# Decay matrices of two DeltaNet pairs made in pieces inside the attention and kept in DRAM, first solve nearer to the attention

## The chip, the cores and the metric

The kernel runs on one core of one Trainium2 chip. The metric is the time of one execution in device microseconds, the median of several runs. A core has TensorE (PE, with its weight loads shown as PEld), VectorE (DVE), ScalarE (ACT), GpSimd (POOL), and SyncE (SP), which here only issues DMA transfers. Each works through its own list of instructions in order and waits on semaphores of the others. Data lies in on-chip SBUF (128 partitions), matmul results in PSUM, and inputs, outputs and spilled tiles in DRAM.

## The reference

One layer of a hybrid backbone, float32, for 512 latent tokens and 256 context tokens of width 1024. Cut to what matters:

```python
hx = modulate(rms_norm(x), sh1, sc1);  hc = modulate(rms_norm(ctx), csh1, csc1)
# (A) softmax attention, 8 query heads, 2 key heads, 512 queries against 256 + 512 keys
# (B) gated DeltaNet, 8 heads, chunks of 64 tokens, forwards and backwards, context first:
gam   = cumsum(log_a)                                  # within a chunk
dec   = exp(where(incl, gam[:, None] - gam[None, :], -inf))
kk    = k @ k.T                                        # within a chunk
a_mat = where(strict, beta[:, None] * dec * kk, 0) + eye(64)
u, w  = triangular_solve(a_mat, [beta * v, beta * exp(gam) * k])
# then a scan over the chunks: delta = u - w @ S;  S = exp(gam_last) * S + k_dec.T @ delta
#                              o = q_dec @ S + (dec * (q @ k.T)) @ delta
y = sigmoid(g_a) * (attn @ w_pa) + sigmoid(g_d) * (gdn @ w_pd);   x = x + g1 * (y @ w_out)
x = x + g2 * conv_ffn(modulate(rms_norm(x), sh2, sc2));  return rms_norm(x)
```

q, k and v of the DeltaNet come out of a projection, a centred convolution of width 3, silu, and for q and k a normalisation by head.

## The kernel before

A float32 matmul is made of three passes over operands split into a high and a low part (whi, wlo for weights; hxH, hxL for the latent and hcH, hcL for the context tokens). wraw is a weight tile as loaded, whi is written by ACT and wlo by VectorE.

The work goes through these stages: modulation and loads (0 to 75 us), projections for the attention (to 153), the attention (to about 325), the DeltaNet (to about 835), and the output projection and the FFN (to the end). Two long lists of independent TensorE work are cut into steps and put between the dependent parts. In the attention it is fillA, the first of the convolution projections (conv_proj, then tokens, which transposes the result co through PSUM tile xb and stores it as kTd, ktd, vtd). Behind it is fill: the other projections, z and gates, the projections pa and pd of the two branches. Asking a list for its next step is a pull; one pull of a projection is three matmuls of 128x512 or six of 128x256 into mb. The lists are fixed, so a pull that isn't taken early is taken later.

The attention (attend) goes through 32 units of 128 queries of one head, numbered u. A unit makes the scores into PSUM tile pS, of which there is one, the row maximum mx (VectorE), the exponentials pm (ACT), the normalisation of pm (VectorE), transposes into ab, their split PH (ACT) and PL (VectorE), and the products with the values. Between these stand pulls of fillA (F0 to F3 of them), and the order of TensorE is pinned as written. ACT, VectorE, POOL and SP are ordered by a scheduler, with contexts such as first() and sooner() as priorities.

The DeltaNet works on pairs of heads, p = 0 to 3. gdn_prep(p) loads k as kT, and makes the decay matrices NN: for each head, row blocks of gamdr are broadcast to all partitions for the two directions (NN and Gb, 128x768 each), POOL or VectorE adds a mask, ACT takes the exponential of six 128x128 pieces of each, and the two are added into NN. gdn_solve multiplies NN by pk = kT times kT and solves the diagonal 32x32 blocks on VectorE (C, X, and a chain of products prod and sums in R), which ends in o_tr and o_nt. gdn_inv makes the whole inverse from these on TensorE (pb), with copies into TTm and Tm on POOL and ACT. gdn_scan runs over the chunks; it loads vtok, ktok and masks M. The order of the first pair is written out:

```python
weave(wait(WK), 1.0)                                          # WK pulls
weave(gdn_solve(pre, G if 0 in SPOOL else V), RK)             # pk, NN times pk, the chain is issued
gdn_solved(pre, False)
weave(wait(W0), 1.0)                                          # W0 pulls, then gdn_inv(0)
```

The scheduler may put operations of gdn_prep ahead of the line at which they are written; their loads start at the attention's end, when the tiles' memory comes free.

Of the kernel before, what the change touches and what calls it, by code (L numbers as in the profile page):

```python
# [6 lines left out]
F32 = mybir.dt.float32  # L7
F32R = mybir.dt.float32r
AF = mybir.ActivationFunctionType
ALU = mybir.AluOpType  # L10
# [4 lines left out]
P = 128  # L15
D = 1024
# [12 lines left out]
NRM = "dve"  # L29
SOLVE = 2500000  # L30
POPS = (1, 3, 5, 7)
CHUNK, WK, W0, W1, RI, RS, RO = 1, 24, 66, 0, 3.0, 2.8, 2.0
RI0 = 2.4
NB = 6 - NX
POOLW = 0
KV = 10
GN = ''
FKS = '4466'
# [39 lines left out]
def hybrid_layer_body(tc, x, ctxt, xT, consts, cols, rows, w_mod1, w_mod2, w_av, w_aq, w_cm, w_pa, w_pd, w_out,  # L78
                      w_up, w_down, outT, dbg=None):
    nc = tc.nc  # L80
    V, A, G, SP = nc.vector, nc.scalar, nc.gpsimd, nc.sync
# [20 lines left out]
    def dump(name, ap):  # L102
        if dbg is not None and name in dbg:
            SP.dma_start(dbg[name], ap)

    def tt(out, a, b, op, eng=None):
        (eng or V).tensor_tensor(out=out, in0=a, in1=b, op=op)  # L107

    def ts(out, a, s1, op0, s2=None, op1=None, eng=None):
        if op1 is None:  # L110
# [5 lines left out]
        V.scalar_tensor_tensor(out=out, in0=a, scalar=s, in1=b, op0=op0, op1=op1)  # L116

    def act(out, a, f=AF.Copy, **kw):
        A.activation(out, a, f, **kw)  # L119

    def split(hi, lo, src):
        act(hi, src)
# [10 lines left out]
    with es:  # L133
        cp = es.enter_context(tc.tile_pool(name="cp", bufs=1))
        dp = es.enter_context(tc.tile_pool(name="dp", bufs=1, space=DRAM))
# [23 lines left out]
        msk_s = (cst[:, C_MS:C_MS + 128], cst[:, C_MS + 128:C_MS + 256])  # L159
# [38 lines left out]
        flat = lambda t: t.rearrange("p a b -> p (a b)")  # L198

        def load_w(src, nk=KT, pool=None, bufs=OH, n=None):  # L200
# [4 lines left out]
            with first() if pool is None else ExitStack():  # L205
                SP.dma_start(raw[:, 0:n], src)
                act(hi[:, 0:n], raw[:, 0:n])
                tt(lo[:, 0:n], raw[:, 0:n], hi[:, 0:n], ALU.subtract, G if pinned[0] and POOLW else V)
            return hi, lo
# [9 lines left out]
        gamdr = dp.tile([96, P], F32, name="gamdr")  # L219
        kTd = [dp.tile([P, NA], F32, name=f"kTd{i}") for i in range(NH)]  # L220
        qTd = [dp.tile([P, NL], F32, name=f"qTd{i}") for i in range(NH)]
        ktd = [dp.tile([P, NA], F32, name=f"ktd{i}") for i in range(NH)]
        vtd = [dp.tile([P, NA], F32, name=f"vtd{i}") for i in range(NH)]
        szd = [dp.tile([P, NL], F32, name=f"szd{i}") for i in range(NH)]
        atd = [dp.tile([P, NL], F32, name=f"atd{i}") for i in range(NH)]

        beta = cr.tile([P, 96], F32, name="beta")
        gam = cr.tile([P, 96], F32, name="gam")
# [201 lines left out]
        with m1_es:  # L430
# [11 lines left out]
            for op in LORD.split():  # L442
                i = int(op[1])
                with sooner():
# [3 lines left out]
                    elif op[0] == "h":  # L448
                        h, part = order[i]
# [312 lines left out]
        with at_es:  # L762
            at2 = at_es.enter_context(tc.tile_pool(name="at2", bufs=1, reuse_waits="tile"))
# [49 lines left out]
            def softmax(h, t, pS):  # L813
# [9 lines left out]
                    norm(pm, mx[:, 3:4])  # L823
                return pm

            def attend():
                U = 4 * NH
                at = lambda u: (u // 4, u % 4)
                pS, pms, pv = scores(0, 0), {}, None
                yield F0  # L830
                for u in range(U + 2):
                    if u < U:
                        pms[u] = softmax(*at(u), pS)
                    if u + 1 < U:
                        pS = scores(*at(u + 1))
                    yield F1
                    if pend:
                        columns(*pend.pop(0), xbank()[:, 0:2, :])
                    nxt = None
                    if 0 < u <= U:  # L840
                        nxt = probs(*at(u - 1), pms.pop(u - 1))
                    yield F2
                    if pv is not None:
                        pv()
                    yield F3
                    pv = nxt
# [30 lines left out]
        def gdn_prep(p, eng=G):  # L877
            kT = gq.tile([P, 2, NA], F32, name="kT", align_bytes=2048, tag="kT", bufs=2)
            for hh in range(2):
                SP.dma_start(kT[:, hh, :], kTd[2 * p + hh])  # L880
            g = gq.tile([P, 32], F32, name="g", tag="g", bufs=2)
            gT = gq.tile([P, 32], F32, name="gT", tag="gT", bufs=2)
            V.memset(g[:, 24:32], 0.0)
            for d in range(2):
                for hh in range(2):
                    r0 = d * 48 + (2 * p + hh) * 6
                    u = slice(12 * d + 6 * hh, 12 * d + 6 * hh + 6)
                    stt(g[:, u], beta[:, r0:r0 + 6], -1.0, rkk[2 * p + hh], ALU.mult, ALU.mult)
                    tt(g[:, u], g[:, u], rkk[2 * p + hh], ALU.mult)
            V.transpose(gT, g)  # L890
            NN = gq.tile([P, 12, P], F32, name="NN", align_bytes=2048, tag="NN", bufs=2)
            for hh in range(2):
                u = slice(6 * hh, 6 * hh + 6)
                Gb = gq.tile([P, 6, P], F32, name="Gb", tag="Gb", bufs=1)
                for d, D in ((0, NN[:, u, :]), (1, Gb)):
                    r0 = d * 48 + p * 12 + hh * 6
                    SP.dma_start(D.rearrange("p a b -> p (a b)"),
                                 gamdr[r0:r0 + 6, :].rearrange("a b -> (a b)").partition_broadcast(P))
                    tt(D, D, msk_s[d].unsqueeze(1).to_broadcast([P, 6, P]), ALU.add, eng)
                    for c in range(6):  # L900
                        act(D[:, c, :], D[:, c, :], AF.Exp, scale=-1.0, bias=gam[:, r0 + c:r0 + c + 1])
                tt(NN[:, u, :], NN[:, u, :], Gb, ALU.add, eng)
            return [kT, gT, NN]
# [427 lines left out]
        for p in range(NP):  # L1331
# [7 lines left out]
            out = (None, gdn_out(0), gdn_out(1), gdn_reload())[p]  # L1339
# [271 lines left out]
```

## Time and profile before

| | |
|---|---|
| runs | 1258.03, 1258.09, 1261.97 us; median 1258.09 |
| profiled execution | 1256.38 us, span 1254.5 us |
| mean granted clock of TensorE | 0.985 |
| busy: PE, DVE, ACT, POOL | 1196.7, 837.4, 613.8, 274.0 us |
| attention, 200 to 290 us | PE busy 90.00 of 90 us |
| behind it, 325 to 425 us | PE busy 86.10 of 100 us, clock 0.93 |

Times in the profile count from the first instruction. Busy is the sum of an engine's instruction times; a stall of TensorE shows as idle time before an instruction, with the instruction that ended it as releaser. The granted clock is the share of full speed at which the throttle lets TensorE run; at 0.5 a matmul takes twice its time. Line numbers (L107) are those of the kernel, and for helpers that all operations share they are the helper's: L86 matmul, L90 transpose, L107 tensor_tensor (L118 in the changed kernel), L116 scalar_tensor_tensor, L119 activation (L130).

### The profile page before, as it was taken

Reading aid. Unit: us, or ns where it says so; the run is one execution under the profiler, and the core shown is the slowest. Engines: PE = TensorE matmul, PEld = TensorE weight load, DVE = VectorE, ACT = ScalarE, POOL = GpSimd, SP = SyncE. Lnnn points to the kernel's source line nnn. Section 1 sums busy time; section 2 is a strip of 40 time slices with the busy share of each in tenths; the row PEclk is TensorE's granted clock in tenths of the full one; section 3 lists DMA queues with packets and bytes.
Section 4 is the critical chain, followed back from the end, with each engine's and each line's share of the span. In section 5 each row is a group of like instructions: output and inputs, shape, how many; then the busy total and the mean of one; then the engine's idle time right before and its main releaser. Section 6 shows DMA issues by size and latency. Waiting matters only on the chain. (4 is left out here: it accounts for less than half of the span.)

```text
span 1254.5 us, 20509 instructions
## 1 busy us (share of the span) xinstructions
PE 1196.7 (95%) x7733; PEld 1018.3 (81%) x7733; DVE 837.4 (67%) x1609; ACT 613.8 (49%) x1403; POOL 274.0 (22%) x347
## 2 busy tenths in 40 slices
PE   7999999999889899899999999899999999999996
PEld 3599879898778788778888778679888888888886
DVE  5767767777698866766757687855776766653333
ACT  6634466766675673773634632233544444442231
POOL 0120110110422387597484200210000000000000
PEclk9999999999999999999999999999999999999999
DMA  9412311211634533643546786854343332233331
GB/s 377 145 60 85 103 43 60 80 68 60 214 110 162 179 119 115 171 140 107 174 143 192 239 295 210 272 194 135 96 136 122 133 101 101 88 93 96 102 93 67
DMA packets 66403, 171.83 MB, mean 137 GB/s; under 512 B 7328, under 2 KB 18048, under 8 KB 64896
## 3 DMA queue, kind: packets, MB, share of 16 engines
q1 hardware_dynamic: 66304, 170.52, 41.0%
q8 instruction: 61, 1.00, 0.3%
q14 instruction: 38, 0.31, 0.1%
HBM read 145.28 MB, written 25.21 MB: 136 GB/s over the span
## 5 line engine op out<-in xcount | busy, mean ns | idle before, releaser
L107 DVE TENSOR_TENSOR wlo<-wraw,whi 128x1024 fp32r<-128x1024 f32 (+1 forms) x153 | 192.2, 1257 | 155.7 <-ACT whi L119 155.5
L119 ACT ACTIVATE whi<-wraw 128x1024 fp32r<-128x1024 f32 (+1 forms) x153 | 159.6, 1044 | 219.3 <-PE mc L86 112.5
L86 PE MATMUL mc<-h,whi 128*128 128x512 f32 (+1 forms) x752 | 219.7, 376 | 0.3 <-ACT whi L119 0.3
L86 PE MATMUL mb<-hxH,whi 128*128 128x512 f32 x384 | 162.3, 423 | 3.4 <-DVE R L107 2.8
L86 PEld LDWEIGHTS mc<-h,whi 128*128 128x128 f32 x752 | 138.0, 188 | 25.8 <-ACT whi L119 0.5
L86 PE MATMUL mb<-hxH,wlo 128*128 128x512 f32 x384 | 152.6, 397 | 0.0
L86 PE MATMUL mb<-hxL,whi 128*128 128x512 f32 x384 | 151.7, 395 | 0.0
L86 PE MATMUL mc<-h,wlo 128*128 128x512 f32 (+1 forms) x376 | 141.4, 376 | 0.5 <-DVE wlo L107 0.5
L86 PE MATMUL mc<-a,whi 128*128 128x512 f32 (+1 forms) x396 | 111.1, 367 | 0.6 <-DVE x L116 0.6
L107 POOL TENSOR_TENSOR rc<-rc,mhalf 128x2 f32<-128x2 f32 x4 | 3.3, 813 | 407.5 <-DVE rc L113 407.5
L86 PEld LDWEIGHTS mb<-hxH,wlo 128*128 128x128 f32 x384 | 72.9, 190 | 16.5
L86 PEld LDWEIGHTS mb<-hxH,whi 128*128 128x128 f32 x384 | 73.5, 191 | 13.7 <-issue 2.9
L86 PEld LDWEIGHTS mc<-h,wlo 128*128 128x128 f32 x376 | 70.8, 188 | 13.8 <-DVE wlo L107 1.0
L86 PEld LDWEIGHTS mc<-a,whi 128*128 128x128 f32 x396 | 71.6, 189 | 12.8 <-DVE x L116 0.8
L86 PEld LDWEIGHTS mb<-hxL,whi 128*128 128x128 f32 x384 | 73.5, 191 | 9.6
L86 PE MATMUL mc<-a,wlo 128*128 128x512 f32 (+1 forms) x198 | 72.4, 366 | 0.0
L116 DVE SCALAR_TENSOR_TENSOR u<-mc,col,u 128x511 f32<-128x511 f32 x88 | 65.3, 746 | 1.4
L107 POOL TENSOR_TENSOR prod<-X,R 128x31 f32<-128x31 f32 (+15 forms) x93 | 54.4, 584 | 20.6 <-DVE X L107 13.9
L107 POOL TENSOR_TENSOR R<-R,prod 128x31 f32<-128x31 f32 (+15 forms) x93 | 57.1, 614 | 7.0
L86 PE MATMUL pq<-whi,hxH 128*128 128x256 f32 (+1 forms) x192 | 55.6, 290 | 0.0
L86 PE MATMUL pq<-wlo,hxH 128*128 128x256 f32 (+1 forms) x192 | 54.4, 283 | 0.1
L86 PE MATMUL pq<-whi,hxL 128*128 128x256 f32 (+1 forms) x192 | 54.3, 283 | 0.0
(329 smaller groups left out, 2768.1 us busy)
## 6 DMA issues: line engine op xcount, KB each, us to landing
wraw<-in_w_cm_dram SPq DMA_DIRECT2D x48, 512.0 KB, 3.6
wraw<-in_w_up_dram SPq DMA_DIRECT2D x44, 512.0 KB, 3.3
wl<-in_w_mod_dram SPq DMA_DIRECT2D x24, 512.0 KB, 4.6
wm<-in_w_mod_dram SPq DMA_DIRECT2D x8, 1024.0 KB, 10.7
wraw<-in_w_down_dram SPq DMA_DIRECT2D x16, 512.0 KB, 3.5
wraw<-in_w_aq_dram SPq DMA_DIRECT2D x10, 512.0 KB, 3.7
M<-gamdr SPq DMA_DIRECT2D x64, 64.0 KB, 4.9
wraw<-in_w_pa_dram SPq DMA_DIRECT2D x8, 512.0 KB, 4.4
```

The costliest lines, as they stand in the source:

```text
L86: i = nc.tensor.matmul(*a, **k)
L107: (eng or V).tensor_tensor(out=out, in0=a, in1=b, op=op)
L116: V.scalar_tensor_tensor(out=out, in0=a, scalar=s, in1=b, op0=op0, op1=op1)
L119: A.activation(out, a, f, **kw)
```

## The change

The NN matrices of the first ND = 4 heads (pairs 0 and 1) are made during the attention, in tiles of their own, NN0 and Gb0 (NN_2056 and Gb_2057 in the rows below). Each head has two broadcast loads and two masks on POOL, then six pieces of two exponentials (DN = 2), one piece per unit, then a merge on POOL and a store to a DRAM tile nnd. These instructions are pinned in the order written. gdn_prep then loads NN of these heads from nnd and makes no masks or exponentials for them. WK goes from 24 to 10 and W0 from 66 to 60.

```diff
-CHUNK, WK, W0, W1, RI, RS, RO = 1, 24, 66, 0, 3.0, 2.8, 2.0
+CHUNK, WK, W0, W1, RI, RS, RO = 1, 10, 60, 0, 3.0, 2.8, 2.0
...
+ND, DN = 4, 2
...
+    def put(i):
+        return tc.keep_in_program_order(i) if strict[0] else i
...
+    def in_order(fn, *a):
+        strict[0] = True
+        fn(*a)
+        strict[0] = False
...
-        (eng or V).tensor_tensor(out=out, in0=a, in1=b, op=op)
+        put((eng or V).tensor_tensor(out=out, in0=a, in1=b, op=op))
...
-        A.activation(out, a, f, **kw)
+        put(A.activation(out, a, f, **kw))
...
+        nnd = [dp.tile([P, 6 * P], F32, name=f"nnd{i}") for i in range(ND)]
...
+            def decays():
+                NN = at2.tile([P, 6, P], F32, name="NN0")
+                Gb = at2.tile([P, 6, P], F32, name="Gb0")
+                rows6 = lambda d, h: slice(d * 48 + h * 6, d * 48 + h * 6 + 6)
+                def masks(D, d, h):
+                    SP.dma_start(D.rearrange("p a b -> p (a b)"),
+                                 gamdr[rows6(d, h), :].rearrange("a b -> (a b)").partition_broadcast(P))
+                    tt(D, D, msk_s[d].unsqueeze(1).to_broadcast([P, 6, P]), ALU.add, G)
+                def decay(D, d, h, c0):
+                    for c in range(c0, c0 + DN):
+                        kc = rows6(d, h).start + c
+                        act(D[:, c, :], D[:, c, :], AF.Exp, scale=-1.0, bias=gam[:, kc:kc + 1])
+                def merge(h):
+                    tt(NN, NN, Gb, ALU.add, G)
+                    SP.dma_start(nnd[h], NN.rearrange("p a b -> p (a b)"))
+                for h in range(ND):
+                    yield 0, lambda: masks(NN, 0, h)
+                    yield 0, lambda: masks(Gb, 1, h)
+                    yield 1, lambda: None
+                    for D, d in ((NN, 0), (Gb, 1)):
+                        for c in range(0, 6, DN):
+                            yield 1, lambda: decay(D, d, h, c)
+                    yield 0, lambda: merge(h)
+            pieces, left = decays(), [0.0]
+            def decay_pieces():
+                left[0] += 1
+                while left[0] > 0:
+                    share, fn = next(pieces, (99, None))
+                    left[0] -= share
+                    if fn:
+                        in_order(fn)
...
+                        decay_pieces()
...
+                if 2 * p + hh < ND:
+                    SP.dma_start(flat(NN[:, u, :]), nnd[2 * p + hh])
+                    continue
```

ACT in the attention, before: a unit's splits PH, then pm, with the transposed convolution output co between.

```order
L119 ACTIVATE ao<-ab 128x256
L119 ACTIVATE co<-t_2163 128x768
L119 ACTIVATE PH<-ab 128x4x128
L119 ACTIVATE PH<-ab 128x2x128
L119 ACTIVATE pm,mx<-pS,mx,qsc_174 128x768
L119 ACTIVATE co<-xb,hk_165 128x128 x4
L119 ACTIVATE PH<-ab 128x4x128
L119 ACTIVATE pm,mx<-pS,mx,qsc_174 128x768
L119 ACTIVATE PH<-ab 128x2x128
```

ACT in the attention, changed, over two units.

```order
L130 ACTIVATE PH<-ab 128x4x128
L130 ACTIVATE PH<-ab 128x2x128
L130 ACTIVATE Gb_2057<-Gb_2057,gam 128x128 x2
L130 ACTIVATE pm,mx<-pS,mx,qsc_178 128x768
L130 ACTIVATE ao<-ab 128x256
L130 ACTIVATE co<-t_2175 128x768
L130 ACTIVATE PH<-ab 128x4x128
L130 ACTIVATE PH<-ab 128x2x128
L130 ACTIVATE pm,mx<-pS,mx,qsc_178 128x768
```

A piece of two exponentials now stands behind the PH splits of a unit; in 11 of the 24 units with a piece it is directly ahead of pm, in the others behind it.

TensorE around pk, before: pk of pair 0 stands behind a whole projection of the context.

```order
L86 MATMUL mb<-hcH,whi 128x256
L86 MATMUL mb<-hcL,whi 128x256
L86 MATMUL mb<-hcH,wlo 128x256
L86 MATMUL pk<-kT 128x128 x4
L86 MATMUL mb<-hxH,whi 128x512
L86 MATMUL mb<-hxL,whi 128x512
L86 MATMUL mb<-hxH,wlo 128x512
L86 MATMUL pk<-kT 128x128 x2
```

TensorE around pk, changed.

```order
L91 MATMUL xb<-cst,co 128x128 x2
L87 MATMUL pk<-kT 128x128 x4
L87 MATMUL mb<-hcH,whi 128x256
L87 MATMUL mb<-hcL,whi 128x256
L87 MATMUL mb<-hcH,wlo 128x256
L87 MATMUL mb<-hcH,whi 128x256
L87 MATMUL mb<-hcL,whi 128x256
L87 MATMUL mb<-hcH,wlo 128x256
L87 MATMUL pk<-kT 128x128 x2
```

pk stands 14 pulls nearer to the attention, inside the projection that stood ahead of it; between pk and the inverse there are six pulls and six transposes fewer.

POOL ahead of and in the inverse of pair 0, before: all masks of M, then the copies of the inverse.

```order
L107 TENSOR_TENSOR M_5230<-M_5230,cst 128x256 x2
L107 TENSOR_TENSOR M_5241<-M_5241,cst 128x256 x2
L107 TENSOR_TENSOR M_5252<-M_5252,cst 128x256 x2
L107 TENSOR_TENSOR M_5263<-M_5263,cst 128x256 x2
L972 COPY TTm<-o_tr 32x12x32 x4
L972 COPY TTm<-o_nt 32x12x32 x4
```

POOL there, changed.

```order
L118 TENSOR_TENSOR M_5144<-M_5144,cst 128x256
L1027 COPY TTm<-o_tr 32x12x32 x4
L118 TENSOR_TENSOR M_5144<-M_5144,cst 128x256
L118 TENSOR_TENSOR M_5155<-M_5155,cst 128x256 x2
L1027 COPY TTm<-o_nt 32x12x32 x4
L979 MEMSET C 128x32x8
L118 TENSOR_TENSOR M_5166<-M_5166,cst 128x256 x2
L118 TENSOR_TENSOR M_5177<-M_5177,cst 128x256 x2
```

The copies of o_tr and o_nt stand among the masks of M, whose operands come by DMA.

1 line of the change is left out of this document (added).

## The prediction

> **What bounds the kernel now.** I read the stretches of the span first, then the waits of TensorE, then the work in front of those waits. Columns of the stretch table: length, then busy time (and instructions) of PE, PEld, DVE, ACT, POOL, then the granted clock, the DMA share and GB/s.
>
> ```profile
> 200.00:290.00 90.00, 90.00 (x609) 81.16 (x608) 68.53 (x135) 58.81 (x146) 6.96 (x4) 1.00 0.20 68
> 325.00:350.00 25.00, 21.88 (x122) 18.83 (x120) 15.11 (x46) 19.58 (x64) 11.02 (x6) 0.93 0.68 221
> 325.00:425.00 100.00, 86.10 (x544) 73.12 (x543) 83.40 (x167) 68.87 (x193) 40.46 (x35) 0.93 0.52 170
> 349.40:417.40 68.00, 58.77 (x310) 49.02 (x308) 63.57 (x116) 43.86 (x114) 23.10 (x19) 0.95 0.46 149
> 700.00:775.00 75.00, 70.87 (x477) 59.03 (x476) 60.04 (x129) 26.66 (x54) 0.78 (x1) 1.00 0.80 259
> 900.00:1254.00 354.00, 345.08 (x1595) 288.62 (x1593) 193.11 (x264) 132.13 (x180) 1.39 (x2) 0.99 0.33 106
> ```
>
> TensorE sets the time. Inside the attention (200 to 290) it is never idle, with POOL at 6.96 of 90 us; from 900 on it misses 9 us in 354. Behind the attention, 325 to 425, it is idle 13.9 of 100 us, and a granted clock of 0.93 costs some 7 us more. About 21 us are to be had there. Some of its waits there, and pk (start, duration, instruction; in brackets the idle time before it and its releaser):
>
> ```profile
> 344.24 1.11 PE L90 MATMUL xb<-cst,co 128*128 128x128 f32 x4 [2.94 <-DVE co L116]
> ...
> 348.28 1.05 PE L86 MATMUL pk<-kT 128*128 128x128 f32 x8
> ...
> 364.91 0.76 PE L86 MATMUL mb<-hxH,whi 128*128 128x512 f32 x1 [2.76 <-DVE R L107]
> ...
> 417.43 0.24 PE L86 MATMUL pb<-o_tr,NN 32*32 32x32 f32 x2 [1.12 <-DVE o_tr L952]
> ```
>
> Two halves meet at pk (348.28). Ahead of it the fill's pulls run while ACT and POOL make the decay matrices; the convolution's co stands behind exponentials on ACT, and TensorE waits 2.94 us for the co that follows from it. Behind pk, VectorE runs the solve of pair 0 (NN times pk, X, the R chain, o_tr) with the fill's own VectorE work in between, 63.57 of 68.00 us busy, and the first product of the inverse (417.43) waits for its o_tr. The operations that the change touches, and what they do to VectorE:
>
> ```profile
> 339.69 1.85 ACT L119 ACTIVATE NN<-NN,gam 128x128 f32<-128x128 f32 x6
> 341.45 0.83 ACT L119 ACTIVATE co<-t 128x768 f32<-128x768 f32 x1
> ```
>
> ```profile
> 360.40 1.84 POOL L107 TENSOR_TENSOR NN<-NN,Gb 128x768 f32<-128x768 f32 x1 [2.63 <-ACT Gb L119]
> 366.19 1.82 POOL L107 TENSOR_TENSOR Gb<-Gb,cst 128x768 f32<-128x768 f32 x1 [3.95 <-DMA Gb<-gamdr]
> 371.43 1.84 POOL L107 TENSOR_TENSOR NN<-NN,Gb 128x768 f32<-128x768 f32 x1 [3.42 <-ACT Gb L119]
> ```
>
> ```profile
> 349.98 0.95 DVE L107 TENSOR_TENSOR NN<-NN,Gb 128x768 f32<-128x768 f32 x1
> ...
> 360.57 2.75 DVE L107 TENSOR_TENSOR X<-X,gT 128x1024 f32<-128x1024 f32 x1
> ...
> 371.47 1.98 DVE L107 TENSOR_TENSOR R<-R,prod 128x156 f32<-128x156 f32 x1
> 373.48 0.34 DVE L107 TENSOR_TENSOR prod<-X,R 128x175 f32<-128x175 f32 x1
> ...
> 414.12 1.22 DVE L947 TENSOR_TENSOR R<-R,gT 128x1024 f32<-128x1024 f32 x1
> ```
>
> A VectorE operation that meets a wide one of POOL is held by it: beside the merge at 360.40, X*gT takes 2.75 against the 1.22 of the same shape at 414.12, and beside the one at 371.43 an R step takes 1.98 where a wider step takes 0.34.
>
> **The change part by part.** The sum is made against the profiled execution, 1256.38 us; the median of the runs, 1258.09, stands 1.7 above it.
>
> ```profile
> 204.12 0.87 ACT L119 ACTIVATE PH<-ab 128x512 fp32r<-128x512 f32 x2 [1.77 <-PE ab L90]
> 204.87 0.99 ACT L119 ACTIVATE pm<-pS,mx,qsc 128x768 f32<-128x768 f32 x1
> ```
>
> ```profile
> 204.83 0.39 PE L86 MATMUL mb<-hxH,whi 128*128 128x512 f32 x1
> 205.07 0.39 PE L86 MATMUL mb<-hxL,whi 128*128 128x512 f32 x1
> 205.29 0.40 PE L86 MATMUL mb<-hxH,wlo 128*128 128x512 f32 x1
> 205.52 0.60 PE L90 MATMUL xb<-cst,co 128*128 128x128 f32 x4
> 206.01 0.50 PE L86 MATMUL pS<-KH,QH 128*128 128x512 f32 x1
> ```
>
> *Exponentials in the attention.* Two per unit, 2 x 0.31 = 0.62 us (1.85 for six), in 24 units. ACT has room (58.81 of 90 us), but pS has one buffer: the next scores start when ACT has read pm out of it. In the unit shown pm ends at 205.86 and the scores start at 206.01, a slack of 0.15 us. The new order puts the pair directly ahead of pm in 11 of the 24 units. Units of the shape shown (both PH splits ahead of pm) come once in four, so I count 6 that lose 0.62 - 0.15 = 0.47 us, and nothing for the others, which have ACT's idle time (1.77 us ahead of the PH row) to take it: 6 x 0.47 = +2.8, taken as +3. The ends are 0 and 11 x 0.62 = +7.
>
> *Masks, merges, loads and stores in the attention.* Twelve POOL operations of 1.82 us or more on an engine that is 92% free there cost TensorE nothing of themselves; VectorE can be held by them up to 1.5 us each, and has 21.5 of 90 us idle. I take 0 for them, since only an operation with little slack behind it passes a hold on; the bad end is the rival below. On SP, 8 loads and 4 stores of 384 KB join a stretch with a DMA share of 0.20. A store waits for its merge, and the load of the next weights stands behind it on SP, so that it comes a merge (1.84 us) late at most, four times; no row of the attention shows TensorE short of weights, so 0. The next head's first exponential waits for merge, store, load and mask, whose parts are 1.84 + 2.3 + 6.0 + 1.84 = 12.0 us by the POOL rows and these landings (kTd<-co for a store, kT for a load of the same size, in a crowded stretch). Two units last ten, since a normalisation, one per unit, comes 18 times in 90 us (row below). So ACT may stand 2 us, twice; most units absorb it, and the bounds above hold it.
>
> ```profile
> kT<-kTd SPq DMA_DIRECT2D x4, 384.0 KB, 6.0
> NN<-gamdr SPq DMA_DIRECT2D x4, 384.0 KB, 8.1
> ...
> kTd<-co SPq DMA_DIRECT2D x1, 384.0 KB, 2.3
> ```
>
> *24 pulls to 10 ahead of pk.* A pull is three matmuls, 0.69 us (204.83 to 205.52). pk comes 14 x 0.69 = 9.7 sooner, and the wait of 2.94 goes with the exponentials that caused it, with 1.7 of half clock (0.07 of the 25 us to 350): 14.3, so pk at 333.9. The 24 pulls, that wait and that clock account for 21 us ahead of 348.28, so the attention ends at 325 to 327 and kT and NN have 7 to 9 us to land. The loads above took 6.0 and 8.1 where nine queued; nine queue now, but pk's first products need only kT and the first two of NN. I take no wait.
>
> *pk to the inverse.* It took 417.43 - 348.28 = 69.2. Two bounds. TensorE's own work: 58.77 less 3.4 for the clock of 0.95, plus pk, less 6 pulls and a group of six transposes (5.0), is 51.5. The VectorE chain: 68.0 unchanged at worst; less the two holds shown (1.53 + 1.64), the merge (0.95), some 2 for the fill's VectorE work in six pulls (an estimate: a third of 63.57 us over 66 pulls) and about 4 of other holds, by the mask at 366.19 and the scan's, and of VectorE's 4.4 us of idle time: 58. I take 58, because VectorE was 93% busy there and remains the longer of the two. So the inverse starts at 333.9 + 1.1 + 58 = 393.0, 24.4 sooner. But 20 pulls and six transposes, 13.8 + 0.9 = 14.7 us of TensorE work, have only been moved behind it. Net -9.7; the ends are +0.3 (the chain stays at 68) and -17 (only TensorE's work counts). What is late next is o_tr: TensorE will stand 7 to 8 us before the inverse.
>
> *The inverse and scan 0.* Their fill is 20 pulls nearer, and SP's queue puts the scan's loads behind a store and a load of that fill:
>
> ```profile
> 401.06 6.15 SPq L1034 DMA_DIRECT2D M<-gamdr  x10
> ```
>
> They began 16 us ahead of the inverse; with 14.7 us of fill gone it would be 1 to 2, plus the 7 to 8 of waiting. On POOL the masks of M now stand among the copies TTm<-o_tr and TTm<-o_nt that the inverse needs. The loads fit while TensorE waits. +0.5, ends 0 and +4.
>
> *The tail.* The 20 pulls come out at the end of the fill, beside the projections that move most data (700 to 775: DMA share 0.80, TensorE 4.1 us idle). Another 14.7 us at that stretch's idle share (4.1 of 75) cost 0.8, at five times that share 4; waits of the later projections may go as well: +1, ends -2 and +4.
>
> Sum: +3 - 9.7 + 0.5 + 1 = -5.2: 1251.2 in a profiled execution, 1252.9 as median.
>
> [...]
>
> **The rivals.**
>
> *Slower: POOL holds the attention.* The normalisation of pm stands between softmax and the transposes once a unit:
>
> ```profile
> L111 DVE TENSOR_SCALAR pm<-pm,mx 128x768 f32<-128x768 f32 x18 | 11.2, 621 | 0.6
> ```
>
> It takes 0.62, and no wide POOL operation ran beside it. Stretched to 1.84 in each of the twelve masks and merges, and on the path each time, it would add 12 x 1.2 = 14 us: -5.2 becomes +9, 1267. Without the attention the sum is -8.2, so the kernel gets slower by over 0.3% from 12 us lost in the attention, 0.5 us in each of 24 units. For it: the holds are real. Against it: VectorE has a quarter of its time free there, and POOL would be busy with them 22 of some 120 us, so most normalisations meet none. Chance 0.13, from 1262 up.
>
> *Given back: the chain doesn't shrink.* If VectorE's solve takes its 68 us with less fill to cover it, the stretch gives +0.3 and the sum is +4.8 at the worst, half way back it is 0: 1258 to 1263. For it: the fill's own VectorE work is interleaved by the scheduler and may just close up around the chain. Against: the holds at 360, 366 and 371 have lost their POOL partner. Chance 0.17.
>
> *More: TensorE's work alone counts.* If the chain ends within the fill, -17 with the attention (+3), the tail (+1) and the M loads (0.5 to 4) is -9 to -12.5: 1245.6 to 1249. Chance 0.25.
>
> **How the numbers follow.** Forecast 0.45, with a range of its own from 1249 to 1257. From the four cases: faster by over 0.3% (3.8 us, about what a measurement of this kernel can tell) is all of the larger gain and two thirds of the forecast, 0.57; within 0.3%, 0.25; slower by more, most of the contention case and a part of the giving back, 0.18. The range, 1243 to 1261, takes in the forecast, the larger gain and the giving back, and leaves out the contention case.
>
> **What would show it.** Right: 24 pairs of exponentials on ACT in the attention, TensorE waiting for pm some 0.5 us in a few units and otherwise full; pk about 14 us sooner, with no wait for co ahead of it; X*gT at 1.22; one wait of 5 to 9 us for o_tr ahead of the inverse. Wrong: normalisations of 1.2 us and more beside POOL rows; a wait for NN from nnd; waits for TTm or M inside the inverse; new waits for weights between 780 and 840.

## The result, and the profile after

| | median us | runs | range |
|---|---|---|---|
| before | 1258.44 | 7 | 1256.84 to 1262.52 |
| changed | 1267.33 | 7 | 1264.15 to 1270.71 |

The changed kernel is slower by 0.6%: the ratio is 1.0062, with an interval of 1.004 to 1.0085. 1252.9 was forecast. The profiled execution took 1269.64 us (span 1267.6), 2.3 above its median, and that of before 1256.38 (span 1254.5), 2 below its own; so about 9 of the 13.1 us between the spans are the change. In the experiments below, disturbed executions (one each of m_place and s_swap_16_74) are left out.

TensorE does the same work (busy 1196.8 us, before 1196.7), so the 13 us are idle time and must be looked for stage by stage. The stage table of the changed kernel; columns are the length, busy time and count of PE, PEld, DVE, ACT, POOL, then granted clock, DMA share, GB/s. The stages are the attention, its end to inverse 0, inverse 0 to inverse 3, inverse 3 to the output projection, and the rest:

```profile
153.44:333.54 180.10, 169.41 (x1117) 149.35 (x1117) 133.81 (x246) 123.41 (x330) 38.34 (x24) 0.99 0.27 91
333.54:402.20 68.66, 59.19 (x357) 51.31 (x355) 58.50 (x150) 39.34 (x102) 14.90 (x12) 0.97 0.53 182
402.20:678.74 276.54, 265.35 (x2281) 227.45 (x2281) 186.25 (x358) 151.70 (x405) 183.24 (x267) 0.98 0.44 139
678.74:844.96 166.22, 149.41 (x993) 122.81 (x993) 112.12 (x212) 60.94 (x135) 24.02 (x22) 0.97 0.69 230
844.96:1267.60 422.64, 412.33 (x2035) 349.72 (x2033) 234.90 (x342) 160.13 (x228) 5.11 (x5) 0.99 0.34 109
```

The same of before:

```profile
153.56:325.31 171.75, 167.47 (x1117) 150.13 (x1117) 125.67 (x246) 110.52 (x282) 16.70 (x12) 0.98 0.19 68
325.31:417.43 92.12, 79.74 (x426) 67.36 (x424) 78.11 (x160) 62.86 (x177) 34.12 (x25) 0.94 0.52 169
417.43:688.48 271.05, 261.57 (x2268) 224.68 (x2268) 186.68 (x359) 147.74 (x390) 179.05 (x263) 0.99 0.46 148
688.48:831.78 143.30, 134.75 (x936) 110.08 (x936) 107.21 (x208) 53.36 (x122) 21.22 (x19) 0.99 0.75 245
```

The stages changed by +8.3, -23.5, +5.5, +22.9 and -0.1 us. The counts of matmuls say how much of this is work that only moved: the second stage has 69 fewer, the third 13 and the fourth 57 more. A fill matmul starts 0.23 us after the one before (three take 0.69 us, 204.83 to 205.52, in the profile of before), so 13.1 of the fourth stage's 22.9 us are moved work. The third stage's 13 are three fill matmuls and ten transposes of 0.1 us (four take 0.36 us, 414.32 to 414.68, in the profile of before), about 1.7 us of its 5.5. What is new is 8 us in the attention, 10 us in the fourth stage and 4 us in the third, against the 9 that the second stage gained beyond its moved work. In the fourth stage TensorE's busy time grows by 14.7 us (149.41 against 134.75) for 13.1 of moved work, so 1.5 of its extra 9.8 us are longer matmuls and 8.3 are idle time.

The steps at TensorE, from the timeline of the changed kernel (start, duration, instruction, in brackets the idle time before and its releaser):

```profile
341.30 0.94 PE L87 MATMUL pk<-kT 128*128 128x128 f32 x7
...
402.20 0.31 PE L87 MATMUL pb<-o_tr,NN 32*32 32x32 f32 x2 [7.58 <-DVE o_tr L1007]
...
683.32 0.25 PE L87 MATMUL pb<-o_nt,NN 32*32 32x32 f32 x1 [4.33 <-DVE oacc L118]
...
785.03 0.92 PE L91 MATMUL pb<-cst,oacc 128*128 128x128 f32 x4 [2.23 <-DVE oacc L122]
...
821.19 0.71 PE L87 MATMUL mb<-g_s,whi 128*128 128x512 f32 x2 [4.37 <-DVE gd L127]
```

pk comes 7.8 us behind the attention's end without a wait, and the first product of the inverse waits 7.58 for o_tr, as forecast. The last three rows are waits of the fourth stage, which held 8.55 us of idle time before and 16.81 now.

### The profile page after: what moved, and what is told of

The parts are those of the page before. It is cut to its first block, busy times and chain, and to the rows that moved or that the text cites. A ratio compares the mean times of both kernels' runs of the same rounds, so it can differ in the third digit from the quotient of the medians.

```text
span 1267.6 us, 20507 instructions
## 1 busy us (share of the span) xinstructions
PE 1196.8 (94%) x7733; PEld 1017.4 (80%) x7733; DVE 830.4 (66%) x1603; ACT 614.4 (48%) x1403; POOL 283.0 (22%) x353
## 4 chain that ended last, share of the span: by engine, by line
PE 73%; DMA 8%; DVE 7%; ACT 5%; POOL 3%; issue 3%; SPq 1%; POOLq 0%; DVEq 0%; ACTq 0%
PE mc L87 32%; PE mb L87 19%; PE pq L87 6%; PE pb L87 6%; PE pS L87 2%; PE ab L87 2%; DMA NN<-gamdr 2%; POOL NN L118 1%; PE pm L87 1%; DMA Gb<-gamdr 1%; DMA wl<-in_w_mod_dram 1%; DVE wlo L118 1%; DMA gt<-atd 1%; PE ab L91 1%; ACT pm L130 1%
## 5 line engine op out<-in xcount | busy, mean ns | idle before, releaser
L118 DVE TENSOR_TENSOR wlo<-wraw,whi 128x1024 fp32r<-128x1024 f32 (+1 forms) x153 | 189.6, 1240 | 163.8 <-ACT whi L130 156.3
L87 PE MATMUL mb<-hxL,whi 128*128 128x512 f32 x384 | 152.9, 398 | 0.0
L87 PEld LDWEIGHTS mb<-hxH,whi 128*128 128x128 f32 x384 | 74.1, 193 | 10.6
L87 PEld LDWEIGHTS mc<-a,whi 128*128 128x128 f32 x396 | 71.6, 189 | 12.9 <-DVE x L127 0.8
L118 POOL TENSOR_TENSOR R<-R,prod 128x31 f32<-128x31 f32 (+15 forms) x93 | 59.9, 644 | 6.7
```

The lines of the kernel that those rows point to most:

```text
L87: i = nc.tensor.matmul(*a, **k)
L118: put((eng or V).tensor_tensor(out=out, in0=a, in1=b, op=op))
```

## The experiments

Each profile was cut into the same stages. The table has stage lengths of one profiled execution each, the matmuls of the fourth stage in brackets, and the time: median and ratio to before, or one execution where no ratio stands.

| kernel | attention | to inverse 0 | to inverse 3 | to output projection | us | ratio |
|---|---|---|---|---|---|---|
| before | 171.8 | 92.1 | 271.1 | 143.3 (936) | 1258.4 | |
| changed | 180.1 | 68.7 | 276.5 | 166.2 (993) | 1267.3 | 1.0062 |
| a_fill_only | 170.5 | 84.6 | 277.1 | 165.3 (994) | 1278.0 | 1.0151 [1.0103, 1.0199] |
| b_masks_only | 177.6 | 80.3 | 273.1 | 143.0 (937) | 1255.6 | 0.9971 [0.995, 0.9992] |
| c_w0_80 | 179.1 | 84.1 | 267.9 | 143.9 (936) | 1254.7 | 0.9969 [0.995, 0.9988] |
| d_w1_5 | 179.2 | 68.6 | 280.8 | 153.9 (948) | 1261.2 | 1.0019 [1.0002, 1.0036] |
| e_swap | 177.0 | 81.0 | 271.5 | 145.2 | 1254.1 | 0.997 [0.9946, 0.9993] |
| f_no_pool | 176.1 | 89.2 | 273.4 | 145.7 | 1262.8 | |
| g_no_exp | 176.2 | 91.0 | 273.3 | 143.1 | 1262.7 | |
| h_w0_70 | 179.1 | 70.5 | 279.4 | 160.6 (965) | 1265.2 | 1.0049 [1.0028, 1.007] |
| j_no_wl_loads | 179.4 | 68.7 | 274.9 | 156.0 (993) | 1256.2 | |
| k_w0_80_no_wl_loads | 178.9 | 84.7 | 268.8 | 137.9 (936) | 1250.9 | |
| m_place | 178.8 | 81.9 | 273.8 | 146.1 | 1256.5 | 0.9977 [0.9954, 0.9999] |
| n_dma_only | 175.9 | 90.1 | 273.5 | 143.7 | 1260.7 | |
| o_no_m_loads | 179.1 | 71.6 | 278.2 | 162.9 (993) | 1269.2 | |
| p_w0_80_no_m_loads | 177.3 | 86.7 | 265.6 | 148.1 | 1254.7 | |
| q_dve | 180.2 | 80.1 | 272.1 | 142.6 | 1258.9 | 1.001 [0.9989, 1.0031] |
| r_dve_place | 186.6 | 81.1 | 276.2 | 143.8 | 1261.9 | 1.0034 [1.0016, 1.0052] |
| s_swap_16_74 | 179.2 | 86.2 | 269.9 | 144.0 | 1260.6 | 1.0022 [1.0002, 1.0042] |
| t_w0_90 | 179.0 | 91.1 | 267.2 | 150.8 (906) | 1266.6 | 1.0074 [1.0051, 1.0096] |

**The two parts apart.** First the moved fill without the early matrices:

```diff
-ND, DN = 4, 2
+ND, DN = 0, 2
```

> Only the fill is shifted (10 and 60 pulls); no decay matrix is made in the attention, so masks and exponentials stand behind it as before. Segments of the changed kernel against before, by the profiles: attention 180.1 against 171.9 us; from its end to the inverse of pair 0 68.7 against 92.1, of which 14.7 are fill moved to the end, so a gain of 8.8; from the first inverse to that of pair 3 5.5 more; from there to the first matmul of the output projection 22.9 more, 14.7 of it moved fill, so a loss of 8.2. Theory 1 (the shifted fill is what costs behind the inverse: 5.5 + 8.2): the attention takes 172, the two later segments lose 10 to 14, the stretch ahead of the inverse gains at most 4, so 1264 to 1268 us. Theory 2 (those losses come from the early matrices and their traffic, or from one unlucky profile): the later segments lose under 4, 1256 to 1261.

1278.0 us, 1.5% slower: the moved fill alone costs more than the whole change. Its stage table, from the attention's end to the output projection:

```profile
324.92:409.54 84.62, 66.00 (x357) 56.96 (x355) 69.62 (x155) 53.30 (x150) 25.84 (x17) 0.90 0.49 162
409.54:686.66 277.12, 265.73 (x2280) 227.62 (x2280) 187.23 (x359) 152.01 (x407) 183.82 (x270) 0.98 0.44 142
686.66:851.91 165.25, 151.04 (x994) 123.97 (x993) 113.09 (x213) 59.86 (x134) 23.02 (x20) 0.96 0.68 229
```

With the decay matrices still made behind the attention, the first stage shown is 84.62 us with 66.00 of PE: pk's products wait 5.48 and 4.27 us for VectorE's product with NN, waits that before's profile doesn't have. Its attention is no longer than before's, and its last two stages are within 1 us of the changed kernel's. So the loss behind inverse 0 comes from the moved fill, without the early matrices.

Then the early matrices without the moved fill:

```diff
-CHUNK, WK, W0, W1, RI, RS, RO = 1, 10, 60, 0, 3.0, 2.8, 2.0
+CHUNK, WK, W0, W1, RI, RS, RO = 1, 24, 66, 0, 3.0, 2.8, 2.0
```

> Only the early decay matrices; the pulls stay 24 and 66, so no fill is moved. Theory 1: the attention still takes 8 more, the stretch to the inverse takes 78 to 81 us in place of 92 (the chain of some 59 us behind pk, pk at 20), and nothing behind it changes: -3 to -6, 1252 to 1256. Theory 2: the losses of 5.5 and 8.2 behind the inverse come back here, 1262 to 1270. A third reading (the attention's 8 us are only in that one profile) would show 172 there and 1245 to 1248.

1255.6 us, a ratio of 0.9971. The stage table, the second and the fourth:

```profile
331.23:411.57 80.34, 74.35 (x426) 63.21 (x424) 64.97 (x154) 49.59 (x131) 21.41 (x19) 1.00 0.55 181
...
684.69:827.70 143.01, 133.12 (x937) 108.98 (x936) 107.00 (x209) 53.74 (x123) 20.97 (x18) 1.00 0.75 246
```

The second stage does the work of before (426 matmuls) in 80.34 us instead of 92.12, at full clock; the attention pays 5.8 of these 11.8 us. The fourth stage is as it was.

**How far the fill may move.** In the changed kernel, WK + W0 = 70 pulls stand ahead of inverse 0, before 90. These take 80, 90 and 100, the extra pulls standing between pk and the inverse:

```diff
-CHUNK, WK, W0, W1, RI, RS, RO = 1, 10, 60, 0, 3.0, 2.8, 2.0
+CHUNK, WK, W0, W1, RI, RS, RO = 1, 10, 70, 0, 3.0, 2.8, 2.0    # h_w0_70
+CHUNK, WK, W0, W1, RI, RS, RO = 1, 10, 80, 0, 3.0, 2.8, 2.0    # c_w0_80
+CHUNK, WK, W0, W1, RI, RS, RO = 1, 10, 90, 0, 3.0, 2.8, 2.0    # t_w0_90
```

> The early matrices and the early pk (10 pulls), but 80 pulls behind it, so that no fill is moved past the inverse. TensorE has 70 us of work to the inverse, the chain ends at 12 + 61 = 73 us: the wait for o_tr of 7.6 us should be nearly gone, under 3 us. Theory 1: attention +8, stretch 73 to 75 (-17 to -19), nothing behind it: 1247 to 1251, faster than before. Theory 2: 13 more, 1260 to 1264.

> The changed kernel with 70 pulls behind pk in place of 60, so that 10 pulls in place of 20 are moved past the inverse. The sum of 10 and 60 gave 1267, that of 10 and 80 gave 1254.7. If each moved pull costs its cover, gradually: 1259 to 1262, the segment behind inverse 3 at 152 to 156 us of which 7 are moved work. If the loss is a matter of a few alignments (loads of M ahead of inverse 3, the last projections), it is either nearly all there or nearly gone: 1265 or more, or 1256 or less.

> The changed kernel with 10 and 90 pulls, so 10 pulls are moved forward past the old place, ahead of the inverse. Pulls ahead of the inverse, 70, 80 and 90 in all, gave 1267, 1265.2 and 1254.7. If the waits of the scans and the last projections grow with every pull they lack, the curve goes on, less the 7 us that TensorE does sooner and the chain no longer hides: from inverse 0 to the end 5 to 10 less than with 90 once the moved work is taken off, 1250 to 1254. If the step between 80 and 90 is one threshold and nothing lies beyond it: 1254 to 1257. If the old place is a tuned optimum on both sides: 1258 and more.

70, 80, 90 and 100 pulls gave 1267.3, 1265.2, 1254.7 and 1266.6 us. Of these four, 90 is the best: 80 keep three quarters of the loss, and 100 bring it back. With 90 the early pk remains, the 20 pulls are back ahead of the inverse, and the kernel is faster than before's and than the changed one. With the matmuls counted off at 0.23 us, the fourth stage differs from before's by +9.8 (70 pulls), +10.6 (80), +0.6 (90) and +14.4 us (100): work that is moved out of it (906 matmuls with 100 pulls) makes it longer too. The fourth stage of t_w0_90:

```profile
690.80:841.60 150.80, 134.65 (x906) 109.14 (x906) 107.01 (x208) 50.98 (x118) 21.00 (x19) 0.92 0.68 228
```

TensorE is idle 16 us here against 8.55 before, and the clock falls to 0.92. So the amount of work in this stage doesn't decide its loss. I read it as a matter of which step of the fill stands beside which dependent step; no run changes one such pair alone. c_w0_80 has a new wait too, in its timeline of TensorE:

```profile
408.77 0.69 PE L91 MATMUL xb<-cst,co 128*128 128x128 f32 x2 [6.25 <-ACT co L130]
```

ACT's exponentials of M and copies into Tm stand ahead of co there. The wait is 6.26 in t_w0_90 and 4.63 in s_swap_16_74, which divides the 90 pulls 16 to 74 (on e_swap below) and is 6 us slower than with 24 and 66 or 10 and 80, most of it in the stage to inverse 0 (86.2 us against e_swap's 81.0) and in the attention. So 90 pulls in all are not enough either; their division counts as well:

```diff
+CHUNK, WK, W0, W1, RI, RS, RO = 1, 16, 74, 0, 3.0, 2.8, 2.0
```

> Early matrices with swapped tiles, 16 and 74 pulls, 90 in all as before: pk 8 pulls sooner than with 24 and 66. If pk's place decides when the inverse starts, the stretch from the attention's end falls from 81.0 to 75 to 78 and the time from 1254 to 1249 to 1252; if TensorE's own 71 to 74 us of work and one wait bound it either way, it stays within 2 us of 1254. No fill is moved past the inverse, so nothing behind it should change by more than 3 us.

Five pulls behind each scan take the moved work out of the end of the fill instead:

```diff
+CHUNK, WK, W0, W1, RI, RS, RO = 1, 10, 60, 5, 3.0, 2.8, 2.0
```

> The changed kernel with 5 pulls behind each of the four scans: the 20 moved pulls are spent before the last projections. Theory 1, in the form that the loss of 8.2 us comes from 20 more pulls at the end, where loads are dense: the segment behind inverse 3 falls by 14 to 20 us against the changed kernel, those ahead of it take 10 to 14 more: 1260 to 1264. If it is not the place of the pulls but the waits of the scans themselves: as the changed kernel, 1265 to 1270.

1261.2 us: the fourth stage has 45 matmuls fewer than in the changed kernel (10.4 us) and gets 12.3 us shorter, while the third, which has taken them, gets only 4.3 longer, since there they fill idle time. About two thirds of the loss come back, by another place for the same work. The fourth stage itself still loses 7.8 us against before with its moved matmuls counted off; what came back is the third stage's.

**What the last projections wait for.** The waits of the changed kernel between inverse 3 and the output projection have this line (us in total, times, longest):

```profile
DVE wl L395 <- DMA wl<-in_w_mod_dram: 10.7, 7, 3.4
```

And of before:

```profile
DVE wl L383 <- DMA wl<-in_w_mod_dram: 6.8, 4, 2.3
```

wl are weights of the FFN's modulation, made on VectorE in pinned places, so VectorE stands until each load is in. Two kernels leave these loads out (wl is made from cw), one on the changed kernel and one on c_w0_80:

```diff
-SP.dma_start(wl, w_mod2[j])
-...scalar_tensor_tensor(out=wl, in0=wl, ...
+...scalar_tensor_tensor(out=wl, in0=cw, ...
```

> The changed kernel without the 24 loads of wl (512 KB each) at the end of the DeltaNet; the VectorE operations that used them stay, on resident data, so the modulation of the FFN is wrong. For the segment from inverse 3 to the output projection: 143.3 us before, 166.2 in the changed kernel, of which 13 to 14 are moved work. Theory W (VectorE stands in its pinned operation on wl until the load is in, and what TensorE needs stands behind it): the segment falls by 6 to 9 us, to 157 to 160. Theory C (the loss is missing cover for waits on other things): it falls by less than 3.

> The control: 10 and 80 pulls, so no moved fill, also without the 24 loads of wl. The segment was 143.9. Theory W: it falls by 2 to 4, clearly less than in the changed kernel. Theory C: by the same as in the changed kernel.

The fourth stage falls by 10.2 us in the first and by 6.0 in the second. The loads cost both kernels, and the changed one 4.2 us more, as VectorE's waits for them are 3.9 us longer there: some 4 of its 10 extra us. These are single executions, and in the kernels with 24 and 66 pulls this stage by itself takes from 142.6 to 146.1 us, so the 4 us are indicated rather than shown. The same test for M, whose masks wait for their loads inside the inverse (memset instead of four loads per chunk):

```diff
+G.memset(M2, -1.0e4)
...
-for hh in range(2):
-    SP.dma_start(M2[:, d, hh, :], gamdr[cidx(d, hh, c), :].partition_broadcast(P))
```

> The changed kernel without the 96 loads of the scan's masks M (64 KB each); POOL fills M with a constant instead and the rest stays, so the scan's decays are wrong. In the changed kernel the segment from inverse 0 to inverse 3 takes 276.5 us (before 271.1, no fill moved there), and that behind inverse 3 still loses some 9 us, of which the loads of wl explained 4. Theory M (loads of M come late on SP's queue behind the moved fill, and POOL and ACT, in order, hold the copies of the inverse and the fill's whi behind them): the waits of 4.3 and 1.0 us in inverse 3 go, so the last segment falls by 4 to 6, and the segment of the scans by 3 to 6. Rival (missing cover on the scan's own dependences): both fall by under 2.

> The control for it, with 10 and 80 pulls (scans 267.9, last segment 143.9) and without the loads of M. Theory M: both segments change by less than 2. Rival: both fall by as much as in the changed kernel.

On the changed kernel the third stage got 1.7 us longer and the fourth 3.3 shorter, on c_w0_80 2.3 shorter and 4.2 longer. The two stages together change by -1.6 and +1.9 us. In the kernels with 24 and 66 pulls, where no fill was moved, the third takes from 271.1 to 276.2 us and the fourth 142.6 to 146.1, so shifts of this size come with any new arrangement: the loads of M don't explain the loss. (POOL has one operation more per chunk here, the memset.)

**What the attention lost.** f_no_pool keeps the traffic and the exponentials and leaves out masks and merges; g_no_exp leaves out the exponentials; n_dma_only leaves out both. All three stand on b_masks_only and make their matrices behind the attention as before, so only their attention is compared.

```diff
-tt(D, D, msk_s[d]..., ALU.add, G)                # f, n
-tt(NN, NN, Gb, ALU.add, G)                       # f, n
-act(D[:, c, :], ..., AF.Exp, scale=-1.0, ...)    # g, n: left out
+act(D[:, c, :], ..., AF.Exp, scale=0.0, ...)     # f
-if 2 * p + hh < ND:
+if 2 * p + hh < 0:
```

> Only for the attention's segment (171.8 before, 177.6 with the early matrices): loads, 24 pairs of exponentials and stores stay in the attention, the twelve masks and merges on POOL are left out (the exponentials have scale 0), and the matrices that the solve uses are made behind the attention as before. Theory A (exponentials in front of pm make the loss): 176 to 178. Theory P (VectorE held by POOL): 172 to 173.5.

> The counterpart: loads, twelve masks and merges on POOL and stores stay in the attention, the 24 pairs of exponentials are left out there, and the matrices that the solve uses are made behind the attention as before. Theory A: 172 to 173.5. Theory P: 176 to 178. Near 175 in both: the two share the loss.

> Only for the attention's segment: its 8 loads and 4 stores stay, both the POOL operations and the exponentials are left out there (the matrices that the solve uses are made behind it as before). 176.1 without POOL's part, 176.2 without the exponentials, 177.6 with both, 171.8 before. If the two causes are real and merely overlap: 171 to 173. If something common to all three (the traffic, or the pinned order) costs the 4 us: 175 to 176.

I compared the intervals from one unit's scores to the next. From the eighth unit on, their sum exceeds before's by 7.8 us in the changed kernel, 7.0 in b_masks_only, 5.4 in f_no_pool, 4.3 in g_no_exp and 0.0 in a_fill_only and n_dma_only. So the exponentials with the transfers cost 5.4, POOL's work with the transfers 4.3, and together less than the sum. n_dma_only says little on the transfers: nothing holds them back there, so all twelve are issued from 152.9 to 178.0 us, ahead of the eighth unit, and its longer attention is one stop behind this bunch, with a wait of TensorE of 3.79 us for ACT's xb. But f_no_pool has them spread out, the last one at 295.9 us, and its loss repeats every four units as 0.30, 0.14, 0.58 and 0.03 us: the last four intervals, from 297.0 us on, have the same values as the four before them, in which a load and that store run. So the spread transfers cost nothing that the intervals show, and the 5.4 are the exponentials'. Three of four units lose, not one.

POOL's part is seen on VectorE. The normalisation of pm, of the changed kernel, among the groups of instructions (shortest, median and longest ns):

```profile
L122 DVE TENSOR_SCALAR pm<-pm,mx x32: 619/620/2271, 158.3 to 325.0; 128x768 f32<-128x768 f32 x32
```

And of f_no_pool:

```profile
L122 DVE TENSOR_SCALAR pm<-pm,mx x32: 619/621/622, 158.8 to 322.0; 128x768 f32<-128x768 f32 x32
```

Beside POOL's masks and merges a normalisation takes up to 2.27 us, without them never over 0.62. One unit of g_no_exp, where the mask of NN0 runs beside a weight difference (1.21 us elsewhere) and the mask of Gb0 beside an operation of one column, and through it holds pm and the next scores (timeline, all engines):

```profile
198.79 1.85 POOL L118 TENSOR_TENSOR NN<-NN,cst 128x768 f32<-128x768 f32 x1 [7.72 <-DMA NN<-gamdr]
199.03 2.70 DVE L118 TENSOR_TENSOR wlo<-wraw,whi 128x1024 fp32r<-128x1024 f32 x1
...
200.60 2.82 POOL L118 TENSOR_TENSOR Gb<-Gb,cst 128x768 f32<-128x768 f32 x1
...
202.04 1.40 DVE L127 SCALAR_TENSOR_TENSOR mx<-mx,qsc 128x1 f32<-128x1 f32 x1
...
203.47 0.99 ACT L130 ACTIVATE pm<-pS,mx,qsc 128x768 f32<-128x768 f32 x1 [3.49 <-DVE mx L127]
...
204.61 0.50 PE L87 MATMUL pS<-KH,QH 128*128 128x512 f32 x1 [1.80 <-ACT pm L130]
```

The 128x1 operation, 0.16 us in a free unit, ends with the mask of Gb0, and TensorE waits 1.80 us. The hold goes both ways: that mask takes 2.82 us, 1.84 alone. The other way by which POOL reaches TensorE is the round trip of a tile, here in the changed kernel (the rows of all engines that carry it):

```profile
286.77 2.25 POOL L118 TENSOR_TENSOR NN<-NN,cst 128x768 f32<-128x768 f32 x1 [8.86 <-DMA NN<-gamdr]
...
289.06 0.69 ACT L130 ACTIVATE NN<-NN,gam 128x128 f32<-128x128 f32 x2 [2.67 <-POOL NN L118]
...
289.92 0.83 ACT L130 ACTIVATE co<-t 128x768 f32<-128x768 f32 x1
...
290.79 0.96 DVE L127 SCALAR_TENSOR_TENSOR co<-co,t 128x768 f32<-128x768 f32 x1 [3.46 <-ACT co L130]
291.66 0.95 DVE L830 TENSOR_REDUCE mx<-pS 128x1 f32<-128x768 f32 x1
...
292.84 0.99 ACT L130 ACTIVATE pm<-pS,mx,qsc 128x768 f32<-128x768 f32 x1 [0.75 <-DVE mx L127]
...
293.98 0.50 PE L87 MATMUL pS<-KH,QH 128*128 128x512 f32 x1 [1.52 <-ACT pm L130]
```

NN0 is read by merge and store, then loaded again; its mask waits 8.86 us for the load, ACT stands 2.67 for the mask with co behind it, VectorE 3.46 for that co with the row maximum behind it, though its scores were long done; so pm is late, and TensorE waits 1.52 for it. e_swap lets the two tiles change places for each head, so that the load of the next head's first matrix doesn't wait for the store:

```diff
 yield 0, lambda: merge(h)
+NN, Gb = Gb, NN
```

> The early matrices with pulls 24 and 66, and the two tiles change places after each head: the next head's first load goes into the tile that the merge has read, and need not wait for the store of the other. Theory R (the wait of ACT for mask, load and store of the same tile is a good part of the attention's 6 to 8 us; in the changed kernel it is one unit with a wait of 1.5 and an interval longer by 2.3): the attention falls from 177.6 to 174 to 175.5, and the time by 2 to 3, 1252.5 to 1254. If that wait is covered: no change, 177 to 178 and 1255 to 1257.

1254.1 us, the lowest median of all; but the attention takes 177.0 us, as if the wait had been covered, and its excess from the eighth unit on falls only from 7.0 to 6.3. The interval against before excludes 1, but b_masks_only, c_w0_80 and e_swap can't be told apart by it.

m_place moves the piece behind pm (on e_swap), to test whether the pair ahead of pm is what costs:

```diff
                         pms[u] = softmax(...)
+                        decay_pieces()
...
-                        decay_pieces()
```

> The kernel with swapped tiles (pulls 24 and 66), the piece of exponentials called behind softmax in a unit, so that ACT does it right behind pm in place of ahead of it (11 or 12 units ahead of pm become 1). Theory A (a pair ahead of pm delays the next scores): the attention falls from 177 to 173.5 to 175, the time from 1254 to 1251 to 1252.5. If the loss comes from ACT being behind wherever the pair stands: 176 to 178, time unchanged within 1 us.

The excess is 5.9, against 6.3, and no time is gained. The sum hides two changes. From 280 to 301 us, where none of POOL's masks and merges runs, four intervals lose 0.30, 0.11, 0.00 and 0.00 us instead of f_no_pool's 0.30, 0.14, 0.58 and 0.03, so the pair costs less behind pm. Other units lose more, the most, 1.63 us, beside two of POOL's masks, and take the gain back. q_dve (on e_swap) and r_dve_place (on m_place) give masks and merges to VectorE:

```diff
-tt(D, D, msk_s[d].unsqueeze(1).to_broadcast([P, 6, P]), ALU.add, G)
+tt(D, D, msk_s[d].unsqueeze(1).to_broadcast([P, 6, P]), ALU.add)
...
-tt(NN, NN, Gb, ALU.add, G)
+tt(NN, NN, Gb, ALU.add)
```

> Swapped tiles, pulls 24 and 66, and the twelve masks and merges of the attention on VectorE in place of POOL (about 0.95 us each, 11 us on an engine that is a quarter idle there). The intervals between scores from the eighth unit on were longer than before by 5.4 us with the exponentials alone, 4.3 with POOL alone, 6.3 to 7.8 with both. If POOL's holds are the price, not the work itself: the excess falls to 5 to 6 and the time to 1252 to 1254. If 0.95 us of VectorE hurt as much wherever they fall: 7 to 9, 1255 to 1257.

> The same with the exponentials called behind softmax. With that order alone the excess was 5.9, of which 3 to 4 lay where POOL was busy; two of the four units of each head lost nothing. With POOL out of it the excess should be 2.5 to 4.5, the time 1250 to 1253. If the exponentials cost the same wherever they stand: 5 to 6.

The excess rises to 8.0 and 12.6 us. With its holds, POOL is still the cheaper place for work that is pinned in this order. The 0.95 us of an operation are not the whole price: from 195 to 335 us VectorE, in order, also stands 3.7 and 5.1 us in front of these operations until their loads are in.

## Why the prediction was wrong

*The stretch behind the attention: right.* Forecast -9.7 net of moved work, measured -23.5 + 14.7 = -8.8. The parts fit as well: pk 7.8 us behind the attention's end (8.6 forecast), 60.9 from pk to the inverse (59.1), 7.58 waiting for o_tr (7 to 8), and X*gT freed of its hold:

```profile
354.14 1.21 DVE L118 TENSOR_TENSOR X<-X,gT 128x1024 f32<-128x1024 f32 x1
```

So the rivals "the chain doesn't shrink" and "TensorE's work alone counts" both fell.

*The tail: the step that failed.* "+1, ends -2 and +4" for 20 pulls at its idle share; it was 22.9 - 13.1 = +9.8, and +8.6 in a_fill_only. The step took moved matmuls as costing their own length and a share of idle time. The runs show that its place counts more: 80, 90 and 100 pulls ahead of the inverse gave +10.6, +0.6 and +14.4. Of the +9.8, 8.3 are idle time of TensorE and 1.5 longer matmuls: the clock stands at 0.50 from inside the wait of 4.33 us to 688.9, and from 822.0 to 825.4 behind that of 4.37, where a 128x512 matmul took 0.63 us instead of 0.39. A pull that goes back shifts every later pairing of fill and dependent work, such as the product of inverse 3 that now waits 4.33 for oacc and the last projections that wait for VectorE's wl and gd; that these pairings are the cause is my reading of the waits. For one of them, the loads of wl, single executions indicate about 4 of the 10 us; the loads of M did not account for the rest, and no other single dependence was isolated. That the moved fill costs these 10 us is shown; by which dependences it does so stays open.

*The attention: the size was off.* "+3, ends 0 and +7" became +8.3. Two terms: the exponentials cost 5.4 instead of 2.8, since three of four units lose rather than the one I had looked at; and POOL's work, put at 0, costs 4.3 by itself, 1.6 to 2.4 on top of the exponentials (b_masks_only and the changed kernel against f_no_pool). The evidence against the rival (21.5 of 90 us of VectorE idle) was an average: a hold matters where VectorE's operation is on the way to pm. In the unit of g_no_exp above VectorE runs without a pause from the weight difference to the normalisation. In the changed kernel four of the 32 normalisations took 2.27, 2.17, 1.18 and 1.02 us beside POOL's masks and merges, the other 28 0.62. The rival, "slower: POOL holds the attention", was right on this mechanism and wrong on its size: it decides from 12 us, and the attention lost 8.3. b_masks_only, which has all of it, is faster than before.

*The inverse and scans: +0.5 forecast, +5.5 measured,* of which 1.7 are moved work. One part that was left out is the clock behind the wait of 7.58 us. The ten us from the inverse's first product, of the changed kernel and then of before:

```profile
402.00:412.00 10.00, 8.27 (x213) 7.05 (x213) 3.84 (x7) 5.60 (x14) 9.17 (x16) 0.65 0.25 60
```

```profile
417.00:427.00 10.00, 8.05 (x217) 7.05 (x218) 7.69 (x11) 7.46 (x21) 6.34 (x10) 0.83 0.53 165
```

In the changed kernel the clock is at 0.50 from 398.7 to 409.0 us, 10.2 us of which 3.5 lie in the wait itself; before, from 419.1 to 422.5, 3.4 us, behind waits of 1.12 and 1.52 us with two products between them. At 0.50 the eight products of pk took 2.08 us (405.47, changed) and a 128x512 matmul of the fill started every 0.43 us; at 1.00 it was 1.05 us (348.28, before) and 0.23. What decides how long the clock stays there, no run isolates.

The price is smaller than the clock alone says, since TensorE waits for VectorE at first in any case (1.53 us). Counted to the same product, the first of Y (pb<-Y,o_nt), the changed kernel needs 8.76 us from the start of the inverse and before 7.94: 0.8 us. The other 3 us no run explains; they are within the 5 us by which this stage differs among kernels with 24 and 66 pulls (271.1 to 276.2).

The sum of the steps was -5.2. With the tail's +9.8, the attention's +8.3 and the scans' +3.8 against the stretch's -8.8 it is +13.1, which is what the two spans differ by. The forecast had the mechanism that it looked at right, and priced what it moved as if it had no place. Of its signs all those for the stretch came, and with them two of being wrong: normalisations of over 1.2 us beside POOL rows, and new waits between 780 and 840 us, though of TensorE for oacc and gd and not for weights.

## What to carry to other kernels

Independent work that covers a dependent chain has a place as well as a length: before moving it, look at what it covers where it stands, what it would stand against where it goes, and try some counts on both sides, since the best may be narrow. When a change has two parts, time them apart: here one part gained 0.3%, the other lost 1.5%, and the early matrices without the moved fill (24 and 66 pulls, or 10 and 80) were the version to keep. An engine's average idle time says little on an operation that the critical path waits for; look at the slack of that operation, in every phase of the loop rather than in one unit.

## What the runs showed of the hardware

- POOL operations of 128x768 (1.84 us alone) and VectorE operations beside them lengthened each other: the normalisation took up to 2.27 us for 0.62 in the changed kernel, and in g_no_exp a 128x1024 difference 2.70 for 1.21, a 128x1 operation 1.40 for 0.16, and the POOL mask beside it 2.82.
- Eight loads and four stores of 384 KB cost TensorE nothing that the intervals of f_no_pool show while they are spread over the attention. Issued within 25 us, in n_dma_only, they came with one wait of 3.79 us.
- Behind a wait of 7.58 us the granted clock stood at 0.50 for 6.8 us more, and the same product came 0.8 us later than behind one of 1.12 us.
